# The projection of the second attention branch, rebuilt around single-operand work on VectorE

## The chip, the cores and the metric

The kernel runs on one core of a Trainium2 chip. The engines that matter are TensorE (PE, the matmuls; PEld is its weight load), VectorE (DVE), ScalarE (ACT), GpSimd (POOL) and SyncE (SP), which here issues most of the DMAs; ACT issues the rest from its own instruction stream. SBUF is the on-chip memory that all engines read and write; PSUM is the memory, in eight banks, into which TensorE accumulates. The metric is the device time of one execution in microseconds.

## The reference

One layer of a streaming encoder: 1024 prompt frames and 64 sample frames (1088 columns in all, written T below) of 1024 channels.

```python
h = rms_norm(x, norm_w) @ w_in          # 6144 columns: q, k, v, z of two branches, then g_sb, g_cb
b_sb = (o_sb * silu(z_sb)) @ w_proj_sb  # o_sb: stick-breaking attention, 8 heads x 64
b_cb = (o_cb * silu(z_cb)) @ w_proj_cb  # o_cb: chunk-band attention, 8 heads x 64
y = x + (sigmoid(g_sb) * b_sb + sigmoid(g_cb) * b_cb) @ w_out
```

The first branch is called sb, the second cb. Each projection has 512 input channels and 1024 output channels. All values are float32.

## The kernel before

**Arithmetic.** TensorE multiplies a rounded 32-bit type (fp32r). Each float32 operand x is therefore split into a high part xh (x rounded, written by ACT as a copy) and a low part xl = x - xh (a subtraction on DVE or POOL), and each product is three matmuls: whi by xh, whi by xl, wlo by xh. The parts of a weight block are made by `W.split`: high by ACT (L107), low by POOL (L114).

**Stages.** The input projection comes first (matmuls at L453, and L622 in products of half-size blocks). Then attention: for every stick-breaking or chunk-band tile TensorE makes scores (L994, L995), transposes weights (L1046) and multiplies values (L1085), while ACT takes exponentials (L1004) and DVE normalises (L1018) and copies transposes out of PSUM (L1057). TensorE would idle between these, so a generator hands it "fill" matmuls in between: first the last units of the input projection (L758, with their gate columns g_sb and g_cb passing through ACT, L733, and to DRAM, L675), and then the sb projection (L883), whose results DVE multiplies by the gate (L888). The order within each engine is the order in which the code is written; a tile framework adds the waits. `fill(n)` hands out n further matmuls, or all that are left.

**The two projections.** One generator, `proj_units`, does both. It walks 24 steps: output unit pair i (0 to 3), column chunk ci (`CH`: 384, 384 and 320 of the T columns) and unit uu (0, 1). A unit is 128 output channels. Each step is 12 matmuls into one PSUM tile. For sb the pair is (2i, 2i+1), for cb it is (i, i+4). The gates come back from DRAM in tiles of one unit, 128x384, issued from ACT's stream (L842), three or seven steps ahead; the sb gates are already sigmoids, those of cb get their sigmoid on ACT (L847). For sb the product goes from PSUM into `tbt`, the sum of both branches (1024 channels by T). For cb DVE multiplies PSUM by the gate into SBUF (L891), POOL adds that onto `tbt` (L892), and then the parts for the output projection are made: `keep_h` makes high (ACT, L911) and low (DVE, L913) of the finished columns, three steps behind.

**Sums.** The output projection (matmuls L1337) multiplies by `w_out` in two column halves i, each as seven block products and one b step instead of eight, in the order `OP_`. It needs differences of quarters of `tbt`. `sums_h(k)` makes four of them for the channel pair k: differences into an SBUF tile d (DVE, L923), high part (ACT, L924), low part (DVE, L928). k = 0, 1 run during cb; k = 2, 3 after it. The block weights are made by `prep_o` (ACT L1236, low part on POOL or DVE L1237, sums of weight blocks L1220, L1228). The 64 sample columns take their own matmuls (L1372) from `hs` (L1264, L1265). Results leave by L1360 and L1294.

**Memory.** `x` and its parts live in four tiles of 128x4xT; when x is dead, `tbt` and the parts of the merged value take their places. The cb input (attention output times gate, parts `og`) is made from `ot` tiles loaded by SP (L813) with ACT L817 and DVE or POOL L822. In PSUM the cb units use two banks of `acc` and four of `b`.

Of the kernel before, what the change touches and what calls it, by code (L numbers as in the profile page):

```python
# [17 lines left out]
KT = 8  # L18
# [14 lines left out]
def hybrid_step_kernel(ctx: ExitStack, tc: tile.TileContext, x_prompt, x_sample, c_sbk, c_sbv, c_cbk, c_cbv,  # L33
# [94 lines left out]
    xhl = [[xpool.tile([128, 4, T], F32R, name=f"x{s}{h}") for h in range(2)] for s in "hl"]  # L128
# [622 lines left out]
    def run_fill():  # L751
        for j, (kind, c, args) in enumerate(units):
            wh, wl = W.sp.pop(("u", j))
            for ci, (a, b) in enumerate(CH):
                ps = psF.tile([128, 512], F32, name="acc")
                for k in range(KT):
                    for n, (w, x) in enumerate(((wh, 0), (wh, 1), (wl, 0))):
                        TE.matmul(ps[:, :b - a], w[:, k], xk(x, k)[:, a:b], start=k == 0 and n == 0,  # L758
                                  stop=k == KT - 1 and n == 2)
                        if ci == k == n == 0 and j + 1 == len(units):  # L760
                            load_og("sb", 0, late["y"])
                        if ci == 1 and k == 0 and n == 0:
# [13 lines left out]
        late["tbt"] = [xpool.tile([128, 4, T], F32, name=f"x{s}1") for s in "hl"]  # L776
        late["tbx"] = ExitStack()
        late["tbp"] = late["tbx"].enter_context(tc.tile_pool(name="tbp", bufs=1, side="right"))
        g = proj_units("sb", late["tbp"], 4)
        next(g)  # L780
        next(g)
        for i, v in enumerate(g):
            yield v
            og_step(i % 3 == 2)
# [3 lines left out]
    def og(b, s, p):  # L788
        return xk(s, p) if b == "sb" else late["og"][s][:, p]

    def tb(u):
        return late["tbt"][u // 4][:, u % 4]
# [16 lines left out]
    def load_og(b, ci, stage, ps=range(NPAIR)):  # L809
        a, e = CH[ci]  # L810
        for p in ps:
            ots[ci, p] = stage.tile([128, 384], F32, name="ot", bufs=4)
# [17 lines left out]
    def proj_units(b, pool, ng):  # L830
        gts = {}
        pair = [(2 * i, 2 * i + 1) if b == "sb" else (i, i + 4) for i in range(KT // 2)]
        order = [(i, uu, ci) for i in range(KT // 2) for ci in range(3) for uu in range(2)]

        def load_g(x):
            if x < len(order):
                i, uu, ci = order[x]
                u = pair[i][uu]
                a, e = CH[ci]
                gts[x] = (late["y"].tile([128, 384], F32, name="ot", bufs=4) if b == "cb" and x & 4  # L840
                          else pool.tile([128, 384], F32, name="gt", bufs=4))
                A.dma_start(gts[x][:, :e - a], d_g[b][u][:, a:e])  # L842

        def sig(x):
            if b == "cb" and x < len(order):
                a, e = CH[order[x][2]]
                A.activation(gts[x][:, :e - a], gts[x][:, :e - a], AF.Sigmoid)  # L847

        nxt = [0]

        def load_to(n):
            while nxt[0] < n:
                load_g(nxt[0])
                nxt[0] += 1

        load_to(min(ng - 1, 4))
        yield 0
        if b == "cb":
            W.split(("p", 5))
        sig(0)  # L860
        yield 0
        for x, (i, uu, ci) in enumerate(order):
            u = pair[i][uu]
            i += 0 if b == "sb" else 4
            wh, wl = W.sp["p", i]
            a, e = CH[ci]
            n = e - a
            cw = slice(uu * 128, uu * 128 + 128)
            if x % 6 == 0:
                load_proj(i + 2)  # L870
            if x % 6 == 0 and i != 4:
                if i + 1 < 8:
                    W.split(("p", i + 1))
                else:
                    late["o"](0)
            sig(x + 1)
            gt = gts.pop(x)
            nm = [None, None, "b20", "b21", "b30", "b31"][x % 6] if b == "cb" else None
            ps = late["psB"].tile([128, 512], F32, name=nm) if nm else psF.tile([128, 512], F32, name="acc")
            for p in range(NPAIR):  # L880
                gh, gl = og(b, 0, p), og(b, 1, p)
                for m, (w, g) in enumerate(((wh, gh), (wh, gl), (wl, gh))):
                    TE.matmul(ps[:, :n], w[:, p, cw], g[:, a:e], start=p == 0 and m == 0,  # L883
                              stop=p == NPAIR - 1 and m == 2)
                    if p < NPAIR - 1 or m < 2:
                        yield 1
            if b == "sb":
                V.tensor_tensor(out=tb(u)[:, a:e], in0=ps[:, :n], in1=gt[:, :n], op=OP.mult)  # L888
            else:
                h = tb(u)  # L890
                V.tensor_tensor(out=gt[:, :n], in0=ps[:, :n], in1=gt[:, :n], op=OP.mult)  # L891
                G.tensor_tensor(out=h[:, a:e], in0=gt[:, :n], in1=h[:, a:e], op=OP.add)  # L892
                keep.append((u, a, e))
                if len(keep) > 3:
                    keep_h(1, *keep.pop(0))
                if len(keep) > 1:
                    keep_h(0, *keep[-2])
                if x > 7:
                    next(late["t"][(x - 2) // 6 - 1], None)
            load_to(x + ng)  # L900
            yield 1

    keep = []

    def keep_h(s, u, a, e):

        hh, hlo = late["h"][u // 4]
        f = tb(u)
        z = min(e, NP if u >= 4 else 512)
        if a < z and s == 0:  # L910
            A.activation(hh[:, u % 4, a:z], f[:, a:z], AF.Copy)  # L911
# [510 lines left out]
```

## Time and profile before

| What | Value |
|---|---|
| three timed runs, median (lowest to highest) | 1038.21 us (1035.22 to 1039.8) |
| the profiled execution | 1038.12 us, its span 1036.3 us |
| busy TensorE | 996.2 us, 96% of the span |
| busy VectorE | 672.3 us, 65% |
| busy ScalarE / GpSimd | 475.6 us, 46% / 330.1 us, 32% |
| granted TensorE clock, mean | 0.988 |
| DMA | 164.20 MB, mean 158 GB/s |

The span is what the profiler saw of the engines; 1.8 us of the execution lie around it. Times within the profile count from the span's start. In rows of the trace a name such as `gt` is a tile, `d_gsb` a buffer in DRAM; "out<-in" names what an instruction writes and reads. After a row, "[1.9 <-ACT wT L1055]" is the idle time ahead of it on its engine and the instruction that ended it.

### The profile page before, as it was taken

To read this page: it belongs to the slowest core of one execution; us is meant where nothing else is said; L and a number is where in the kernel's file an instruction comes from. 1 tells how busy PE (TensorE), PEld (TensorE's weight loads), DVE (VectorE), ACT (ScalarE), POOL (GpSimd) and SP (SyncE) were. 2 spreads that over 40 slices of the span, in tenths; PEclk is the share of its full clock that TensorE was granted. 3 is DMA by queue.
4 is the path that set the end of the run, shared out by engine and by line. 5 is a ranking of instruction groups with operands and counts; after the bars stand their busy time and mean duration, and the time that the engine had idled before them with its cause. 6 is when DMAs were issued, how large, how long until landed. Compare 5 with 4: busy or idle time off the path is not lost.

```text
span 1036.3 us, 20146 instructions
## 1 busy us (share of the span) xinstructions
PE 996.2 (96%) x7512; PEld 947.9 (91%) x7512; DVE 672.3 (65%) x1246; ACT 475.6 (46%) x1088; POOL 330.1 (32%) x342
## 2 busy tenths in 40 slices
PE   5999999999999999999999999999999999976998
PEld 5999999998999999988989798998988898976998
DVE  5466663885345554198989787566667773799644
ACT  5544432443343333376767575444445433644220
POOL 3376662114354442211111111101004002765632
PEclk9999999999999999999999999999999999998999
DMA  7636468335555332885665474565757635530632
GB/s 239 205 128 207 160 230 285 118 93 163 160 162 177 95 96 85 214 206 156 164 156 159 130 191 135 172 173 166 196 138 226 175 98 175 163 111 29 196 124 80
DMA packets 176114, 164.20 MB, mean 158 GB/s; under 512 B 34512, under 2 KB 162384, under 8 KB 175888
## 3 DMA queue, kind: packets, MB, share of 16 engines
q1 hardware_dynamic: 160384, 145.67, 47.3%
q10 hardware_dynamic: 15632, 17.24, 5.4%
q8 instruction: 59, 0.97, 0.4%
q14 instruction: 39, 0.32, 0.1%
HBM read 104.14 MB, written 58.72 MB: 157 GB/s over the span
## 4 chain that ended last, share of the span: by engine, by line
PE 87%; DVE 6%; DMA 3%; issue 1%; ACT 1%; POOL 1%; SPq 0%; ACTq 0%; DVEq 0%; POOLq 0%
PE acc L453 18%; PE acc L758 17%; PE b L622 15%; PE o L1085 7%; PE b L1337 7%; PE pt L1046 6%; PE acc L883 6%; PE z L995 3%; PE z L994 3%; PE b L883 2%; DVE kp L1014 1%; DMA out_dram<-kos 1%; DMA wrawx<-in_w_in_dram 1%; DVE be L1015 1%; PE pk L338 1%
## 5 line engine op out<-in xcount | busy, mean ns | idle before, releaser
L114 POOL TENSOR_TENSOR wlo<-wraw,whi 128x1024 fp32r<-128x1024 f32 x31 | 75.9, 2449 | 257.0 <-ACT whi L107 220.8
L758 PE MATMUL acc<-xh,wlo 128*128 128x384 f32 (+1 forms) x384 | 130.9, 341 | 0.0
L758 PE MATMUL acc<-xh,whi 128*128 128x384 f32 (+1 forms) x384 | 130.4, 340 | 0.0
L758 PE MATMUL acc<-xl,whi 128*128 128x384 f32 (+1 forms) x384 | 128.6, 335 | 0.0
L1014 DVE TENSOR_TENSOR_SCAN kp<-kp,imp 64x576 f32<-64x576 f32 (+8 forms) x72 | 102.7, 1427 | 21.7 <-ACT kp L997 21.5
L1004 ACT ACTIVATE be<-be,sm 128x640 f32<-128x640 f32 (+5 forms) x72 | 50.7, 705 | 99.9 <-DVE sm L1000 99.9
L1046 PE MATMUL pt<-ident,be 128*128 128x128 f32 (+2 forms) x608 | 90.6, 273 | 6.2 <-DVE wT L1057 3.3
L1055 ACT ACTIVATE wT<-pt 128x512 f32<-128x512 f32 (+3 forms) x130 | 63.5, 502 | 53.8 <-PE pt L1046 53.7
L1046 PEld LDWEIGHTS pt<-ident,be 128*128 128x128 f32 (+2 forms) x608 | 68.8, 140 | 18.2 <-issue 6.4
L453 PE MATMUL acc<-whi,xh 128*128 128x256 f32 x256 | 74.7, 294 | 0.0
L758 PEld LDWEIGHTS acc<-xh,whi 128*128 128x128 f32 x384 | 72.9, 190 | 1.6
L758 PEld LDWEIGHTS acc<-xh,wlo 128*128 128x128 f32 x384 | 72.7, 189 | 1.1
L758 PEld LDWEIGHTS acc<-xl,whi 128*128 128x128 f32 x384 | 72.3, 188 | 0.9
L453 PE MATMUL acc<-wlo,xh 128*128 128x256 f32 x256 | 71.2, 280 | 0.0
L453 PE MATMUL acc<-wlox,xh 128*128 128x256 f32 x256 | 71.2, 280 | 0.0
L453 PE MATMUL acc<-whi,xl 128*128 128x256 f32 x256 | 71.2, 280 | 0.0
L453 PE MATMUL acc<-whix,xh 128*128 128x256 f32 x256 | 71.2, 280 | 0.0
L453 PE MATMUL acc<-whix,xl 128*128 128x256 f32 x256 | 71.1, 280 | 0.0
L1015 DVE TENSOR_TENSOR be<-be,kp 64x576 f32<-64x576 f32 (+8 forms) x72 | 60.3, 837 | 9.6
L997 ACT ACTIVATE kp<-z 128x384 f32<-128x384 f32 (+6 forms) x112 | 54.3, 484 | 24.7 <-PE z L995 23.2
L1085 PE MATMUL o<-wT,vp 128*64 128x256 f32 (+1 forms) x608 | 65.5, 356 | 0.0
L1085 PEld LDWEIGHTS o<-wT,vp 128*64 128x64 f32 x608 | 42.1, 136 | 22.9 <-issue 7.0
(327 smaller groups left out, 3011.8 us busy)
## 6 DMA issues: line engine op xcount, KB each, us to landing
wraw<-in_w_in_dram SPq DMA_DIRECT2D x35, 512.0 KB, 4.4
wrawx<-in_w_in_dram SPq DMA_DIRECT2D x13, 512.0 KB, 4.5
sq<-d_qsbT SPq DMA_DIRECT2D x32, 192.0 KB, 4.2
sq<-d_qcbT SPq DMA_DIRECT2D x32, 192.0 KB, 4.0
xt<-in_x_prompt_dram SPq DMA_DIRECT2D x8, 512.0 KB, 5.4
d_kcbT<-hl SPq DMA_DIRECT2D x8, 512.0 KB, 4.4
d_qcbT<-hl SPq DMA_DIRECT2D x8, 512.0 KB, 5.5
d_ksbT<-hl SPq DMA_DIRECT2D x16, 256.0 KB, 2.6
```

The lines of the kernel that those rows point to most:

```text
L114: (eng or G).tensor_tensor(out=l, in0=raw, in1=h[:].bitcast(F32), op=OP.subtract)
L453: TE.matmul(ps, x, w, start=m == 0, stop=m == len(steps) - 1)
L622: TE.matmul(ps[:, :m], w[:, hl_, k], right[s](x)[:, k, a:b], start=s < 3 and k == 0 and e == 0, stop=k == 3 and e == 2, skip_group_check=s ...
L758: TE.matmul(ps[:, :b - a], w[:, k], xk(x, k)[:, a:b], start=k == 0 and n == 0, stop=k == KT - 1 and n == 2)
L883: TE.matmul(ps[:, :n], w[:, p, cw], g[:, a:e], start=p == 0 and m == 0, stop=p == NPAIR - 1 and m == 2)
L997: A.activation(kp[:r, x:y], z[:r, :m], AF.Sigmoid, scale=-0.125)
L1014: V.tensor_tensor_scan(kp[:r, n - 1::-1], kp[:r, n - 1::-1], im[:, ::-1], 0.0, op0=OP.mult, op1=OP.add)
L1015: V.tensor_tensor(out=be[:r, :n], in0=be[:r, :n], in1=kp[:r, 1:n + 1], op=OP.mult)
L1046: TE.transpose(pt[:kr, x, :r], be[:r, kb * 128:kb * 128 + kr], ident[:r, :r])
L1055: A.activation(w[:, sl:sl + m, q0:q0 + r], pt[:, :m, :r], AF.Copy)
L1085: TE.matmul(o[hd * 64:hd * 64 + 64, c0:c1], vv[:kr, kb, hd * 64:hd * 64 + 64], wT[b, p, j, hd, s // 4][:kr, s % 4, c0:c1], start=si == 0, ...
L1337: TE.matmul(ps[:, t], left[s](xs_)[:, k, ts_], wt_[:, k], start=s < 3 and t == k == e == 0, stop=k == 3 and e == 2, skip_group_check=s > 2 ...
```

## The change

What it does, part by part:

1. **Layout.** The middle two of the four x tiles become one (`xm`), so `tbt` is one tile of 8 units and one operation can cover the units i and i+4. The sb input's parts move to the outer two tiles.
2. **sb.** `proj_sb` walks 12 chunks j = (i, ci) of two units each. The gates come as one tile [128, 2, 384], two buffers, issued by SP (L841) and not by ACT. `load(j + 1)` stands twice in a chunk, at its start and after its first unit; both copies go into one buffer, so the second waits for the first. The weights of the next pair are split in the chunk ci = 1, and not in ci = 0.
3. **cb.** `proj_cb(j)` does a chunk of two units. For ci = 1 and 2 both units lie in one PSUM tile of two banks. DVE multiplies by the gate in place, in PSUM (L910), and then adds `tbt` itself (L911, one operand from PSUM); for ci = 1, 2 each covers two units (128x2x384, 128x2x320). POOL's addition is gone. Gates: two units a tile, four chunks ahead, issued by SP; the sigmoid covers two units.
4. **Low parts.** `keep_lo` (L933) is on POOL, one chunk behind.
5. **Sums.** `sums_h` writes its differences into PSUM. The first two (L950) have both operands in SBUF, the other two (L954, L955) and the four low parts (L947) have one operand in PSUM. k = 0 to 2 run from chunk 3 to 11, k = 3 in `last_sums`, behind the first block product of the output projection.
6. **Weights.** The low part of the second cb weight block goes to DVE. The block sums of the first half of `w_out` are made by POOL (L1284, L1286) in chunks 1 and 2. `OP_` swaps its third and fourth entry; `hs` is one operation of ACT and one of POOL.

The matmuls of TensorE are the same in number. The diff, cut to its core:

```diff
+        load_gate(late["tbp"], "gt", 0, d_g["sb"][0:2], 0)
-        g = proj_units("sb", late["tbp"], 4)
+        late["tbt"] = xpool.tile([128, KT, T], F32, name="xm")
+        for i, v in enumerate(proj_sb(late["tbp"])):
...
+    def load_gate(pool, name, key, us, ci):
+        a, e = CH[ci]
+        gts[key] = pool.tile([128, 2, 384], F32, name=name, bufs=2)
+        for w, d in enumerate(us):
+            SP.dma_start(gts[key][:, w, :e - a], d[:, a:e])
+
+    def proj_sb(pool):
+        load = lambda j: j < 12 and load_gate(pool, "gt", j, d_g["sb"][2 * (j // 3):2 * (j // 3) + 2], j % 3)
+        for j in range(12):
...
+            load(j + 1)
+            if ci == 0:
+                load_proj(i + 2)
+            if ci == 1:
+                W.split(("p", i + 1))
...
+                V.tensor_tensor(out=tb(2 * i + uu)[:, a:e], in0=ps[:, :e - a], in1=gt[:, uu, :e - a], op=OP.mult)
+                if uu == 0:
+                    load(j + 1)
...
+        if ci:
+            ps = late["psB"].tile([128, 2, 512], F32, name=f"b{ci + 1}")
...
+        h = late["tbt"][:, i:i + 5:4, a:e]
+        for x, y, o in (((ps[:, :, :n], gt[:, :, :n], h),) if ci else
+                        [(pp[uu][:, :n], gt[:, uu, :n], h[:, uu]) for uu in range(2)]):
+            V.tensor_tensor(out=x, in0=x, in1=y, op=OP.mult)
+            V.tensor_tensor(out=o, in0=x, in1=o, op=OP.add)
+        load_gcb(j + 4)
-                V.tensor_tensor(out=gt[:, :n], in0=ps[:, :n], in1=gt[:, :n], op=OP.mult)
-                G.tensor_tensor(out=h[:, a:e], in0=gt[:, :n], in1=h[:, a:e], op=OP.add)
...
+                G.tensor_tensor(out=hl, in0=f, in1=hh.bitcast(F32), op=OP.subtract)
-            V.tensor_tensor(out=hlo[:, u % 4, a:z], in0=f[:, a:z], in1=hh[:, u % 4, a:z].bitcast(F32),
-                            op=OP.subtract)
...
     def sums_h(k):
+        d = [psF.tile([128, 512], F32, name="acc")[:] for _ in range(2)]
-            d[n] = late["hp"].tile([128, 512], F32, name="d", bufs=2)
...
+        for j in range(2):
+            V.tensor_tensor(out=d[j], in0=x(j, 1), in1=x(0, j), op=OP.subtract)
+        high(0)
+        yield
+        low(0)
+        V.tensor_tensor(out=d[1], in0=x(1, 1), in1=d[0], op=OP.subtract)
+        V.tensor_tensor(out=d[0], in0=x(1, 0), in1=d[1], op=OP.subtract)
+        yield
+        high(2)
+        yield
+        low(2)
...
-    OP_ = [0, 3, 1, 2, 4, "b", 5, 6]
+    OP_ = [0, 3, 2, 1, 4, "b", 5, 6]
...
+    for j in range(12):
+        proj_cb(j)
+        if j == 0:
+            W.split(("p", 5), V)
+        if j == 1:
+            G.tensor_tensor(out=wsum[3], in0=wsum[0], in1=wsum[1], op=OP.add)
+        if j == 2:
+            G.tensor_tensor(out=wsum[2], in0=wsum[3], in1=wsum[2], op=OP.subtract)
+        if j:
+            keep_lo(j - 1)
+        if j == 11:
+            prep_o(1)
+        else:
+            keep_hi(j)
+        if j > 2:
+            if j % 3 == 0:
+                tjobs = sums_h(j // 3 - 1)
+            if j < 11:
+                next(tjobs, None)
+            if j in (4, 7):
+                next(tjobs)
...
+    def last_sums():
...
+        t3 = sums_h(3)
+        for _ in range(3):
+            next(t3)
+        prep_o(3)
+        keep_hi(11)
+        keep_lo(11)
```

The order of DVE in the middle of the cb projection, before, from the first gate product of a chunk on. `gt` is a gate tile, `b` a PSUM tile with a unit's matmuls, `xl` and `xh` with a number are halves of `tbt` or parts, `h0l` a low part, `d` a difference and th0 to th3 the parts of the differences.

```order
L891 TENSOR_TENSOR gt<-b_11582,gt 128x384
L913 TENSOR_TENSOR h0l<-xh_10320,h0h 128x384
L928 TENSOR_TENSOR th0l<-d,th0h 128x512
L923 TENSOR_TENSOR d<-xl_10321,d 128x512
L891 TENSOR_TENSOR gt<-b_11606,gt 128x320
L913 TENSOR_TENSOR xl_11376<-xl_10321,xh_11375 128x384
L928 TENSOR_TENSOR th1l<-d,th1h 128x512
L923 TENSOR_TENSOR d<-xl_10321,xh_10320 128x512
L891 TENSOR_TENSOR gt<-b_11630,gt 128x320
L913 TENSOR_TENSOR h0l<-xh_10320,h0h 128x128
L928 TENSOR_TENSOR th3l<-d,th3h 128x512
L891 TENSOR_TENSOR ot<-acc,ot 128x384
```

The same place in the change; here `xm` is `tbt`, and `acc` is a PSUM tile with a difference. Two units share an operation, the low parts of the finished columns are gone from DVE, and the additions onto `tbt` and the subtractions with PSUM are there:

```order
L910 TENSOR_TENSOR b_11526<-b_11526,ot 128x384
L911 TENSOR_TENSOR xm<-b_11526,xm 128x384
L910 TENSOR_TENSOR b_11527<-b_11527,ot 128x384
L911 TENSOR_TENSOR xm<-b_11527,xm 128x384
L950 TENSOR_TENSOR acc<-xm 128x512 x2
L910 TENSOR_TENSOR b_11569<-b_11569,gt 128x2x384
L911 TENSOR_TENSOR xm<-b_11569,xm 128x2x384
L947 TENSOR_TENSOR tk_11203<-acc,tk_11203 128x512 x2
L954 TENSOR_TENSOR acc<-xm,acc 128x512
L955 TENSOR_TENSOR acc<-xm,acc 128x512
L910 TENSOR_TENSOR b_11610<-b_11610,gt 128x2x320
L911 TENSOR_TENSOR xm<-b_11610,xm 128x2x320
```

Before, a gate product and low parts alternate, and all but the products have both operands in SBUF; now only the two L950 have.

The gate loads of the sb projection stood in ACT's order before, between the work of attention (L817 copies of the attention output, L1055 copies of transposes, L1004 exponentials) and the weight split (L107):

```order
L842 DMA gt<-d_gsb_93 128x384
L842 DMA gt<-d_gsb_94 128x384
L842 DMA gt<-d_gsb_93 128x384
L107 ACTIVATE whi<-wraw 128x1024
L1055 ACTIVATE wT<-pt 128x3x128
L817 ACTIVATE xh_139<-ot 128x320
L1004 ACTIVATE be,sm<-be,sm 128x640
L817 ACTIVATE xh_139<-ot 128x320
L842 DMA gt<-d_gsb_94 128x384
L1055 ACTIVATE wT<-pt 128x3x128
L817 ACTIVATE xh_139<-ot 128x320
L1004 ACTIVATE be,sm<-be,sm 128x640
```

In the change they stand in SP's order, among the loads of weights (L805) and of the attention's gate `zt` (L1081) and the store of its result (L678). In brackets are the semaphores that an instruction waits for (DMAHW: an earlier transfer has landed; DVE: VectorE has come so far):

```order
L841 DMA gt_10838<-d_gsb4_97 128x384 [waits DMAHW3_49,DMAHW2_49,DVE_49]
L841 DMA gt_10838<-d_gsb5_98 128x384
L841 DMA gt_10874<-d_gsb4_97 128x384 [waits DMAHW4_49,DMAHW3_49,DMAHW2_49]
L841 DMA gt_10874<-d_gsb5_98 128x384
L1081 DMA zt_10890<-d_zcb3_92 128x256
L841 DMA gt_10912<-d_gsb4_97 128x384 [waits DMAHW7_49,DMAHW0_49,DVE_49]
L841 DMA gt_10912<-d_gsb5_98 128x384
L805 DMA wraw_10915<-in_w_proj_cb_dram 128x4x128 [waits DMAHW1_49,Pool_49]
L805 DMA wraw_10915<-in_w_proj_cb_dram 128x4x128
L841 DMA gt_10966<-d_gsb4_97 128x384 [waits DMAHW7_49,DMAHW0_49]
L841 DMA gt_10966<-d_gsb5_98 128x384 [waits DMAHW4_49]
L678 DMA d_ocb3_116<-zt_10744 128x256 [waits DMAHW5_49,DVE_49]
```

Every gate tile is named twice, once for each of the two `load` calls; the second pair waits for the transfers of the first, and what stands behind it on SP waits too.

More of the change, by code (lines that the diff above doesn't have):

```diff
@@ L828, in make_og @@
             og_lo(b, ci, p)
[L830 to L864, printed above, removed]
@@ L880, in proj_units @@
             for p in range(NPAIR):
-                gh, gl = og(b, 0, p), og(b, 1, p)
+                gh, gl = og("cb", 0, p), og("cb", 1, p)
                 for m, (w, g) in enumerate(((wh, gh), (wh, gl), (wl, gh))):
[L883 to L899, printed above, removed]
```

249 lines of the change are left out of this document (144 added, 105 removed).

## The prediction

> **What bounds the kernel now.** I read the table of windows first, by rounds of the cb projection, then TensorE's waits and the chain of waits behind it, then VectorE's groups there. A row of windows gives start:end, length, busy time (and instructions) of PE, PEld, DVE, ACT, POOL, then granted clock, DMA share and GB/s.
>
> ```profile
> 877.70:889.60 11.90, 11.89 (x72) 11.90 (x73) 4.21 (x7) 6.49 (x12) 6.62 (x6) 1.00 0.77 235
> 889.60:901.50 11.90, 11.90 (x74) 11.90 (x73) 10.27 (x16) 7.38 (x17) 10.91 (x9) 1.00 0.55 164
> 901.50:913.50 12.00, 12.00 (x75) 12.00 (x74) 11.93 (x14) 5.73 (x13) 6.58 (x6) 1.00 0.34 104
> 913.50:925.20 11.70, 11.70 (x73) 11.70 (x72) 11.60 (x17) 6.12 (x13) 5.57 (x6) 1.00 0.25 75
> 925.20:956.60 31.40, 17.82 (x117) 16.21 (x115) 30.84 (x33) 13.33 (x26) 16.61 (x11) 0.83 0.16 53
> 956.60:1032.40 75.80, 75.78 (x622) 75.57 (x622) 41.30 (x49) 15.11 (x18) 33.26 (x13) 0.98 0.42 135
> ```
>
> Four rounds of cb keep TensorE full. But from the third on VectorE is full too, and when the rounds end at 925.2 it is still busy to 956.6, while TensorE works 17.82 of 31.40 us at a clock of 0.83. TensorE's waits after 870 us (total, times, longest) say for what:
>
> ```profile
> PE b L1337 <- ACT whio L1236: 4.4, 1, 4.4
> PE b L1337 <- DVE h0l L913: 4.3, 1, 4.3
> PE b L1337 <- POOL wlo L1237: 2.4, 2, 1.8
> ```
>
> ACT had been free before whio; the chain (start, length, what) shows VectorE ahead of it:
>
> ```profile
> 940.98 5.17 DVE xl L913 x2
> 946.15 2.87 DVE hs L1265 x2
> 953.72 0.51 issue
> 954.23 1.05 ACT whio L1236
> 955.31 1.24 DVE wloo L1237
> 956.59 18.58 PE b L1337 x142
> 975.17 0.96 PE acc L1372 x8
> 982.85 11.39 PE b L1337 x96
> 1032.41 0.69 DVE xl L1360
> ```
>
> So the stretch is set by VectorE's backlog. **Its worth:** at full clock a block matmul takes 11.39/96 = 0.1187 us, so 117 of them are 13.9 of the 31.4 us: 17.5 lost. The next 142 took 18.58 where 16.9 would do: 1.7 more. Ceiling 19.2 us. Before 925.2 and behind it TensorE is full, so there is nothing else there.
>
> How the backlog grows is seen from two windows of VectorE, each one round long by its rows:
>
> ```profile
> 901.30:917.70 16.40, 16.30 (x21) 1.00 0.33 100
> 917.70:934.00 16.30, 16.20 (x21) 0.84 0.31 98
> ```
>
> A round costs VectorE 16.3 us and TensorE 11.85 (47.5/4): 4.45 us behind per round. Why so dear is in its groups (busy, mean ns):
>
> ```profile
> L913 DVE TENSOR_TENSOR xl<-xl,xh 128x384 fp32r<-128x384 f32 x8 | 11.4, 1425 | 0.0
> L923 DVE TENSOR_TENSOR d<-xh 128x512 f32<-128x512 f32 x4 | 5.2, 1290 | 0.0
> L928 DVE TENSOR_TENSOR th0l<-d,th0h 128x512 fp32r<-128x512 f32 x4 | 5.2, 1300 | 0.0
> L923 DVE TENSOR_TENSOR d<-xl,xh 128x512 f32<-128x512 f32 x4 | 2.8, 693 | 0.1
> L891 DVE TENSOR_TENSOR gt<-acc,gt 128x384 f32<-128x384 f32 x4 | 2.1, 545 | 0.0
> L891 DVE TENSOR_TENSOR gt<-b,gt 128x320 f32<-128x320 f32 x4 | 1.9, 483 | 0.0
> 917.23 0.55 DVE L913 TENSOR_TENSOR h0l<-xh,h0h 128x384 fp32r<-128x384 f32 x1
> L892 POOL TENSOR_TENSOR xl<-ot,xl 128x384 f32<-128x384 f32 x4 | 5.0, 1246 | 4.7 <-DVE ot L891 4.7
> L114 POOL TENSOR_TENSOR wlo<-wraw,whi 128x1024 fp32r<-128x1024 f32 x3 | 7.2, 2399 | 7.1 <-ACT whi L107 5.3 <-POOL xl L892 1.0 <-DMA gt<-d_gcb 0.8
> ```
>
> The same 384-wide subtraction takes 0.55 us (917.23) or a mean of 1.43; the 512-wide ones 0.69 or 1.3; at 940.98 two L913 took 5.17, about when POOL made weight parts. Those that stretch have two operands in SBUF. The gate products L891, one operand in PSUM, stay at 0.48 to 0.55 in every group.
>
> **A second loss** lies in attention, at 793 us. The windows, then what ACT and TensorE did:
>
> ```profile
> 793.00:796.00 3.00, 1.09 (x8) 0.85 (x7) 0.56 (x2) 2.21 (x4) 1.08 (x1) 0.95 1.09 226
> 796.00:799.00 3.00, 3.00 (x11) 3.00 (x11) 0.56 (x1) 0.47 (x3) 2.12 (x2) 0.50 0.89 272
> 793.41 0.33 ACTq L842 DMA_DIRECT2D gt<-d_gsb  x1
> 793.79 1.06 ACT L107 ACTIVATE whi<-wraw 128x1024 fp32r<-128x1024 f32 x1 [1.66 <-DMA sq<-d_qcbT]
> 795.27 0.44 PE L1046 MATMUL pt<-ident,be 128*128 128x128 f32 x2 [1.91 <-ACT wT L1055]
> 796.19 0.56 DVE L888 TENSOR_TENSOR xh<-acc,gt 128x384 f32<-128x384 f32 x1 [2.49 <-DMA gt<-d_gsb]
> ```
>
> A gate load in ACT's stream waited for a transfer, behind it the weight split and the copy wT, and TensorE for that: 1.9 us idle, then 3.0 us at half clock (1.5 lost): 3.4 us.
>
> **The change part by part.** *VectorE's round of cb.* Removed: five L913 and the eight L923 and L928 in SBUF. New, from chunk 3 on: four 384-wide operations with PSUM (two products, two additions) at 0.545, as L891; two of 768 and two of 640 elements; six 512-wide with one PSUM operand; two L950 with both in SBUF. From L891 at 320 (0.483) to 512 at 0.69 the slope is about 1.09 ns an element, so 768 take 0.97 and 640 take 0.83. Sum 4 x 0.545 + 2 x 0.97 + 2 x 0.83 + 8 x 0.69 = 11.3 us if nothing stretches; with the L950 at L923's 1.29 it is 12.5. No row shows an operation whose result goes to PSUM; nothing excludes that it is as quick as one to SBUF (11.3), and were each of the 14 with PSUM some 0.3 us dearer the round would be 16.3 again. I take 11.9, near the lower end since the nearest rows, L891, never stretched. That equals TensorE's 11.85, so the backlog no longer grows, and the 19.2 us go. The first round, without sums, is 5.8 us: a reserve.
>
> [...]
>
> *POOL* loses its six L892 a round and gets the low parts: three of 384 columns, one of 256 and one of 128, some 5 us by L892's rate (1.25 for 384), and a weight part of 2.4: 7.5 of 11.85, so the cover is ample. It also makes two block sums of some 2.5 us in the first round; both hide there.
>
> *Weight part on DVE in the first round*, 1.23 us as L1237 or 2.5 beside POOL. It stands behind chunk 0 and is wanted at the second round, 12 us on: cost 0 to 2.5, taken 0.5.
>
> *The end of cb.* The last sums (k = 3), the last low parts and the weight part 3 are made behind the last cb matmul. A block takes 48 matmuls, 5.7 us; by `OP_` the fourth, s = 1, is the first to need them all, three blocks and the samples (1.9, twice the 0.96 of the chain) later: 19.0 us. The chain to it: VectorE's tail of the last chunk, ACT's copy of the first block at 5.7, then highs and lows in turn (0.69 each at least on VectorE, two by two, with ACT between), the weight's high 1.05 and its low 2.4 on POOL: by these rows 17 to 20. Cost 0 to 3, taken 0.5.
>
> *The gates of sb on SP.* The 3.4 us at 793 go, as ACT no longer holds a gate load and the first gate is loaded in the last input unit. But each later chunk is loaded twice, and the second copy waits on SP for the first. What is queued behind it are the attention's own loads, and VectorE waits at L865 for both copies. Rows that price it:
>
> ```profile
> 800.23 2.19 SPq L713 DMA_DIRECT2D vs<-d_cbv  x1
> 806.65 0.54 DVE L888 TENSOR_TENSOR xh<-acc,gt 128x384 f32<-128x384 f32 x1
> 857.88 0.49 DVE L888 TENSOR_TENSOR xl<-acc,gt 128x320 f32<-128x320 f32 x1
> gt<-d_gsb ACTq DMA_DIRECT2D x13, 192.0 KB, 2.5
> vs<-in_cache_cb_v_dram SPq DMA_DIRECT2D x1, 256.0 KB, 7.0
> ```
>
> A gate lands 2.5 us after issue. SP is fullest at 797 to 810 (a single issue held it 2.19). Two copies, one behind the other, and four issues (0.33 at 793.41) there put the gates of chunks 1 and 2 at about 805 to 808, while their products were due at 803 to 807; VectorE would be held some 2.6 us twice, with attention's copies behind it, of which TensorE loses 0 to 5. I take 3, nearer the stall at 793, where a hold of ACT of 1.66 cost 3.4. Later a chunk lasts TensorE (857.88 - 796.19)/8 = 7.7 us: enough for two copies.
>
> *Moved at no cost:* the split to ci = 1, hidden by a chunk of 7.7 us (else 2.4 for the part); `OP_`, the single `hs` operation and the merged sigmoid, hidden by ACT at 6 of 12 us a round.
>
> **Sum**, against the profiled execution of 1038.1 us, 0.1 under the median, its span and 1.8 around it: 1038.1 - 19.2 - 3.4 + 0.5 + 0.5 + 3 = **1019.5 us**. By the bounds: all costs nothing 1015.5; all at their upper ends (2.5 + 3 + 5) 1026, and with a round of 12.5, three times 0.65 late, 1028.
>
> **The rivals.** *VectorE still sets the rounds.* If L950 and others stretch to make a round 13.5 to 14.5 us, three rounds leave 5 to 8 us of backlog, and TensorE's clock drops again: 1024.5 to 1029, with the taken costs near their ends 1031. For it: 11.9 has no slack, POOL now makes low parts in the same time. Against: only two of 16 operations can stretch by the rows.
>
> *The second gate copy becomes the bound: slower.* A chunk of sb cannot be shorter than two landings, one behind the other, for there are two buffers: with issue about 1.1 us plus the landing L of the second from when the first is down. At 2.5 that is 3.6 us if the first was issued early, below 7.7 and below the 3.95 of the last four chunks, which TensorE runs alone. But attention's own loads took up to 7.0 us to land in this stretch. At L = 7 eight chunks cost max(0, 8.1 - 7.7) and four 8.1 - 3.95 each: 3 + 17 = 20, all of the gain; that is the point from which it decides. At 8 it is 11 + 21 = 32, and 1052. Against: the 13 gate loads here had a median of 2.5.
>
> *The change doesn't do what it says.* Operations with PSUM stretch too when TensorE is writing other banks or when their result goes there, and a round stays at 16.3: 13.4 of backlog come back, and 1.7 of slow clock: 1034 to 1036.
>
> **How the numbers follow.** Forecast with its costs (1015 to 1024): 0.60. Below 1015, more gone than I saw: 0.09. VectorE still the bound (1024 to 1032): 0.18. No effect: 0.06. Slower by gates: 0.07. What a measurement can tell from no change is 0.5%, 5.2 us: faster below 1033.0, 0.87; within 0.06; slower above 1043.4, 0.07. The range of 1014 to 1031 leaves out no effect and the slower case (0.13) and a little at either end, some 0.05.
>
> **What would show it.** Right: TensorE full from the first cb matmul to the end, no L1337 wait above 2 us, clock 1.00; L910 and L911 at 0.55, 0.83 and 0.97 without spread; a VectorE round of 11.3 to 12.5. The step on the weight part is wrong if TensorE waits for it at the second round, the one on the end of cb if it waits there for a sum or a weight part. The gate step shows in VectorE's L865 waiting for `gt`: twice at about 804 and 808 by my sum, in every chunk by the slower rival. What would make it wrong: a price for PSUM results, which no row shows, and landings under SP's new load.

## The result

| | before | the change |
|---|---|---|
| median (lowest to highest) | 1036.72 us (1034.26 to 1039.8, 4 runs) | 1023.06 us (1021.39 to 1026.16, 4 runs) |
| profiled execution, span | 1038.12 us, 1036.3 us | 1022.21 us, 1020.3 us |
| granted clock, mean | 0.988 | 0.997 |
| busy VectorE / GpSimd | 672.3 / 330.1 us | 654.5 / 322.3 us |

The ratio is 0.987 (95% interval 0.9831 to 0.9909): faster by 13.7 us. The forecast was 1019.5, with a range of 1014 to 1031.

The span falls into pieces at three first matmuls of TensorE: of the sb projection, of cb, and of the output projection. These four numbers are read from the first starts of those lines in each trace, and are used for every run below.

| stretch, us | before | the change | difference |
|---|---|---|---|
| start to first sb matmul | 788.9 | 788.3 | -0.6 |
| sb and the end of attention | 88.8 | 88.4 | -0.4 |
| cb projection | 47.5 | 50.0 | +2.5 |
| output projection to the end | 111.1 | 93.6 | -17.5 |

The first row is not touched by the change; over all runs here it lies between 785.1 and 789.5, so the span of a single profile says little below some 4 us, and the stretches are compared one by one.

The windows of the change, from the first cb matmul on, answer to the first table of the prediction (start:end, length, busy time and instructions of PE, PEld, DVE, ACT, POOL, clock, DMA share, GB/s):

```profile
876.70:890.85 14.15, 12.66 (x76) 12.09 (x74) 7.07 (x11) 7.33 (x12) 4.04 (x5) 1.00 0.86 273
890.85:902.72 11.87, 11.30 (x69) 11.31 (x69) 11.10 (x15) 7.57 (x14) 11.87 (x8) 1.00 0.81 248
902.72:914.58 11.86, 11.86 (x75) 11.86 (x73) 11.65 (x17) 7.41 (x13) 10.47 (x11) 1.00 0.45 140
914.58:926.70 12.12, 12.12 (x76) 12.12 (x75) 11.88 (x18) 7.40 (x13) 7.66 (x7) 1.00 0.18 52
926.70:947.36 20.66, 19.25 (x162) 19.05 (x160) 14.31 (x18) 8.49 (x14) 10.21 (x6) 1.00 0.29 96
947.36:1016.40 69.04, 69.04 (x576) 68.83 (x576) 37.65 (x47) 14.72 (x17) 28.24 (x11) 1.00 0.45 144
```

TensorE no longer falls behind VectorE: the stretch after cb, which took 31.4 us at a clock of 0.83, is gone. VectorE is still full in the rounds (11.65 of 11.86), but it ends them together with TensorE. What TensorE still waits for after 870 us, in all:

```profile
PE b L1394 <- DVE fl L1436: 1.4, 1, 1.4
PE b L905 <- DVE wlo L114: 1.1, 1, 1.1
PE b L905 <- ACT whi L107: 1.0, 1, 1.0
PE acc L861 <- DVE xm L865: 0.5, 1, 0.5
```

VectorE's groups in cb (885 to 930 us; busy, mean ns of one) are the ones that the prediction priced:

```profile
L950 DVE TENSOR_TENSOR acc<-xm 128x512 f32<-128x512 f32 x6 | 7.1, 1226 | 0.0
L947 DVE TENSOR_TENSOR tk<-acc,tk 128x512 fp32r<-128x512 f32 x10 | 6.4, 680 | 0.0
L911 DVE TENSOR_TENSOR xm<-b,xm 128x384 f32<-128x384 f32 x8 | 4.5, 557 | 0.3
L911 DVE TENSOR_TENSOR xm<-b,xm 128x768 f32<-128x768 f32 x4 | 3.8, 957 | 0.1
L911 DVE TENSOR_TENSOR xm<-b,xm 128x640 f32<-128x640 f32 x4 | 3.3, 825 | 0.1
L910 DVE TENSOR_TENSOR b<-b,ot 128x384 f32<-128x384 f32 x4 | 2.2, 556 | 0.0
```

Whatever has an operand in PSUM takes 0.56, 0.68, 0.83 and 0.96 us for 384, 512, 640 and 768 elements. Only L950, with both operands in SBUF, is stretched, to a mean of 1.23; in low_on_dve below, with POOL nearly empty, it is 0.69. In the change's trace TensorE's matmuls write only PSUM tiles, and no row of POOL names a PSUM tile.

### The profile page after: what moved, and what is told of

Same layout as the page of the kernel before. It is cut to its first block, busy times and chain, and to the rows that moved or that the text cites. A ratio compares the mean times of both kernels' runs of the same rounds, so it can differ in the third digit from the quotient of the medians.

```text
span 1020.3 us, 20165 instructions
## 1 busy us (share of the span) xinstructions
PE 990.5 (97%) x7512; PEld 942.2 (92%) x7512; DVE 654.5 (64%) x1233; ACT 473.7 (46%) x1075; POOL 322.3 (32%) x338
## 5 line engine op out<-in xcount | busy, mean ns | idle before, releaser
L114 POOL TENSOR_TENSOR wlo<-wraw,whi 128x1024 fp32r<-128x1024 f32 x30 | 73.9, 2465 | 246.4 <-ACT whi L107 211.3
L761 PE MATMUL acc<-xm,whi 128*128 128x384 f32 (+1 forms) x384 | 129.1, 337 | 0.0
L456 PE MATMUL acc<-whi,xa 128*128 128x256 f32 x256 | 74.7, 294 | 0.0
L761 PEld LDWEIGHTS acc<-xm,whi 128*128 128x128 f32 x384 | 72.5, 189 | 1.0
L456 PE MATMUL acc<-wlo,xa 128*128 128x256 f32 x256 | 71.2, 280 | 0.0
L456 PE MATMUL acc<-wlox,xm 128*128 128x256 f32 x256 | 71.2, 280 | 0.0
L456 PE MATMUL acc<-whi,xm 128*128 128x256 f32 x256 | 71.2, 280 | 0.0
L456 PE MATMUL acc<-whix,xm 128*128 128x256 f32 x256 | 71.2, 280 | 0.0
L456 PE MATMUL acc<-whix,xb 128*128 128x256 f32 x256 | 71.1, 280 | 0.0
L761 PE MATMUL acc<-xa,wlo 128*128 128x384 f32 (+1 forms) x192 | 65.6, 342 | 0.0
L761 PE MATMUL acc<-xa,whi 128*128 128x384 f32 (+1 forms) x192 | 65.6, 342 | 0.0
```

The source lines that it names most:

```text
L114: (eng or G).tensor_tensor(out=l, in0=raw, in1=h[:].bitcast(F32), op=OP.subtract)
L456: TE.matmul(ps, x, w, start=m == 0, stop=m == len(steps) - 1)
```

## The experiments

Two things were to be told apart. Where the gain comes from: my theory is that VectorE's operations with one operand in PSUM are not held up by POOL's work; the rivals are that there are fewer and wider operations, or that POOL simply took work off a full VectorE. And where the three losses come from (2.5 us in cb, the wait for `fl`, and the 3.4 us near 793 that were to go): the second copies of the gates, or something else. All runs below, with the stretches of their profiled execution:

| run | median, us | ratio to before, 95% | sb | cb | output |
|---|---|---|---|---|---|
| the change | 1023.06 | 0.987 (0.9831 to 0.9909) | 88.4 | 50.0 | 93.6 |
| sbuf_product | 1030.8 | 0.9941 (0.9922 to 0.996) | 88.7 | 53.6 | 101.6 |
| sbuf_pool_idle | 1025.48, one run | | 88.8 | 53.7 | 92.0 |
| low_on_dve | 1027.04 | 0.9915 (0.9892 to 0.9937) | 88.2 | 49.1 | 100.0 |
| one_unit | 1023.99 | 0.9871 (0.9849 to 0.9893) | 88.1 | 48.4 | 98.3 |
| one_copy | 1018.57 | 0.9816 (0.9799 to 0.9832) | 88.4 | 47.4 | 93.5 |
| early_split | 1019.01 | 0.9822 (0.9808 to 0.9837) | 88.8 | 49.1 | 93.6 |
| end_swap | 1019.6 | 0.9826 (0.9799 to 0.9853) | 88.0 | 49.5 | 91.8 |
| before_sp (before, one edit) | 1038.6 | 1.0019 (1.0003 to 1.0035) | 89.1 | 47.6 | 110.9 |
| swap_and_one_copy | 1015.9 | 0.9803 (0.9782 to 0.9825) | 87.0 | 47.4 | 91.7 |
| split_on_dve | 1019.42 | 0.9822 (0.98 to 0.9845) | 90.1 | 48.0 | 91.7 |

The change was not timed again beside its variants. The medians of one_copy, early_split, end_swap and swap_and_one_copy lie 1 to 3 us further below it than their cb and output stretches account for, so a difference of medians from the change is read here no finer than some 3 us, and the stretches carry the argument.

### The product in SBUF

```diff
-            V.tensor_tensor(out=x, in0=x, in1=y, op=OP.mult)
-            V.tensor_tensor(out=o, in0=x, in1=o, op=OP.add)
+            V.tensor_tensor(out=y, in0=x, in1=y, op=OP.mult)
+            V.tensor_tensor(out=o, in0=y, in1=o, op=OP.add)
```

> The gate product of cb goes into the gate tile in SBUF, so the addition behind it has two SBUF operands; number and width of the operations are as in the change. If what keeps VectorE quick is the one operand in PSUM, the additions stretch (mean of 384, 768, 640 columns above 0.7, 1.3 and 1.1 us instead of 0.56, 0.97, 0.83), a round of cb takes VectorE 13 to 15 us instead of 11.86, and three rounds late cost 3 to 9 us: 1026 to 1032. If it is that there are fewer and wider operations, the durations stay and the time is 1023 within 1.5.

Measured: 1030.8 us, 7.7 above the change (the profiled execution was the slowest of the four, 1034.54, so its stretches add up to more). The output stretch takes 101.6 instead of 93.6, since VectorE comes out of cb with a backlog again: its round takes 14.44 us (the products at 913.99 and 928.43) instead of 11.86, within the 13 to 15 expected. Its groups (888 to 930 us):

```profile
L911 DVE TENSOR_TENSOR xm<-ot,xm 128x384 f32<-128x384 f32 x4 | 6.7, 1666 | 0.1
L911 DVE TENSOR_TENSOR xm<-gt,xm 128x384 f32<-128x384 f32 x3 | 3.8, 1280 | 0.1
L910 DVE TENSOR_TENSOR ot<-b,ot 128x384 f32<-128x384 f32 x4 | 2.2, 546 | 0.0
L114 DVE TENSOR_TENSOR wlo<-wraw,whi 128x1024 fp32r<-128x1024 f32 x1 | 3.4, 3364 | 0.0
```

The product, still read from PSUM, stays at 0.55; the addition behind it, same width and same number, goes from 0.56 to 1.3 and 1.7. So width and number, which are the same here, are not what keeps the addition short. (The weight part L114 also went from 1.2 to 3.4 us and held TensorE 3.2 us, 2.1 more than in the change. That is 2.1 of the 3.6 us by which cb is longer; single matmuls of cb also take up to 0.52 us, 0.44 in the change, and the mean granted clock of the execution is 0.991 instead of 0.997.)

### The same, with POOL nearly idle

```diff
             V.tensor_tensor(out=y, in0=x, in1=y, op=OP.mult)
             V.tensor_tensor(out=o, in0=y, in1=o, op=OP.add)
...
-                G.tensor_tensor(out=hl, in0=f, in1=hh.bitcast(F32), op=OP.subtract)
+                A.activation(hl, f, AF.Copy)
```

> As the run with the gate product in SBUF, but POOL's low parts are left out of cb: ACT writes a copy in their place (the low parts are wrong by it; all else is computed). POOL is then left with a weight part of 2.4 us a round. If it is POOL's work that stretches operations with two SBUF operands, the additions fall back to 0.6 to 0.8, 1.0 and 0.9 us on the mean for 384, 768 and 640 columns. If SBUF operands are slow by themselves, they stay at 1.3 to 1.7 for 384.

The mean for 384 fell to 0.99 only, between the two theories' numbers, but single rows decide it (start, length, engine and line; first VectorE, then POOL's only operation there):

```profile
912.74 0.56 DVE L911 TENSOR_TENSOR xm<-ot,xm 128x384 f32<-128x384 f32 x1
913.81 2.27 DVE L911 TENSOR_TENSOR xm<-ot,xm 128x384 f32<-128x384 f32 x1
925.09 0.56 DVE L911 TENSOR_TENSOR xm<-gt,xm 128x384 f32<-128x384 f32 x1
926.15 2.26 DVE L911 TENSOR_TENSOR xm<-gt,xm 128x384 f32<-128x384 f32 x1
```

```profile
913.26 2.40 POOL L114 TENSOR_TENSOR wlo<-wraw,whi 128x1024 fp32r<-128x1024 f32 x1 [9.47 <-ACT whi L107]
925.60 2.40 POOL L1259 TENSOR_TENSOR wlo<-wraw,whi 128x1024 fp32r<-128x1024 f32 x1 [9.94 <-ACT whi L1258]
```

Without POOL the two-operand addition takes 0.56, as long as one with PSUM. If it starts while POOL runs, it ends 0.4 us after POOL does (916.08 behind 915.66, 928.41 behind 928.00): it is not slowed, it is held until POOL's operation is over. The products and additions of the change, with an operand in PSUM, are not held: the 32 in cb (L910, L911) lie between 0.555 and 0.967 us, each at the length of its width. Two rows of the change show a product that starts and ends inside the same kind of weight part on POOL:

```profile
919.41 2.41 POOL L1259 TENSOR_TENSOR wlo<-wraw,whi 128x1024 fp32r<-128x1024 f32 x1 [3.97 <-ACT whi L1258]
920.00 0.56 DVE L910 TENSOR_TENSOR b<-b,gt 128x384 f32<-128x384 f32 x1
```

So it is POOL's work, 2.27 us beside it against 0.56 without, and for these operations only where both operands are in SBUF; in the output stretch, 92.0, TensorE no longer waits for VectorE.

### Low parts on VectorE

```diff
-                G.tensor_tensor(out=hl, in0=f, in1=hh.bitcast(F32), op=OP.subtract)
+                V.tensor_tensor(out=hl, in0=f, in1=hh.bitcast(F32), op=OP.subtract)
```

> The change with the low parts of the finished columns on VectorE again, in place of POOL. VectorE had no idle time in rounds 2 to 4 of cb (11.86 us each); five operations with two SBUF operands add 2.5 us a round if they don't stretch (POOL then has only the weight parts) and 5 if they stretch: 3 rounds, 7 to 15 us of backlog, and TensorE waits for it in the output projection: 1030 to 1038. If VectorE was not the bound, as it is 64% busy, the time stays at 1023 within 1.5.

VectorE's groups, 888 to 930 us, and TensorE's waits:

```profile
L933 DVE TENSOR_TENSOR xb<-xm,xa 128x384 fp32r<-128x384 f32 x7 | 6.1, 866 | 0.0
L950 DVE TENSOR_TENSOR acc<-xm 128x512 f32<-128x512 f32 x6 | 3.9, 690 | 0.0
```

```profile
PE b L1394 <- DVE h0l L933: 3.0, 2, 2.6
PE b L1394 <- DVE fl L1436: 2.7, 1, 2.7
```

1027.04, 4.0 above the change and under the range of 1030 to 1038; the output stretch grows by 6.4 us. A settled round of VectorE takes 12.59 us (the products at 909.89 and 922.48) instead of 11.86. The five low parts of that round take 2.35 us, as expected, but with POOL nearly empty the pair of L950 falls from 2.46 to 1.29, which gives 1.2 us a round back; that was left out of the expectation. More of the delay comes from two low parts that POOL's block sum and weight part held in the first rounds: 2.75 us (at 891.32) instead of 0.55, and 1.46 (at 898.39) instead of 0.42. The mean granted clock of the execution is 0.996, against 0.997. So VectorE is the bound of these rounds and has no slack, as its 64% over the whole span would not tell.

### One unit per operation

```diff
-        for x, y, o in (((ps[:, :, :n], gt[:, :, :n], h),) if ci else
-                        [(pp[uu][:, :n], gt[:, uu, :n], h[:, uu]) for uu in range(2)]):
+        for x, y, o in [(pp[uu][:, :n], gt[:, uu, :n], h[:, uu]) for uu in range(2)]:
```

> The change with one unit per operation for all chunks (four more products and four more additions a round, each half as wide). By the trace two of 384 take 1.12 (start to start 1.06) for one of 768 at 0.97 (0.93), two of 320 some 0.96 for one of 640 at 0.83: a round is 0.4 to 0.6 us longer for VectorE, which has no idle time in rounds 2 to 4, so 1.2 to 1.8 us come late and 0 to 2 us are lost: 1023 to 1025. If the width was the main gain, and not the PSUM operand, it is 5 us or more.

The median is 0.9 above the change, with intervals that cover each other. The stretches say more: output 98.3 instead of 93.6 (TensorE's wait for `fl` is 3.2 instead of 1.4), cb 48.4 instead of 50.0. The durations are as expected: a settled round of VectorE takes 12.49 us (the products at 905.55 and 918.04) instead of 11.86. But the first pair of differences with two SBUF operands (L950, here L949) was held by POOL for longer, 4.35 us instead of 2.19; the later pairs take no more than in the change (2.35 against 2.46). The first two pairs, and TensorE's wait:

```profile
893.20 4.35 DVE L949 TENSOR_TENSOR acc<-xm 128x512 f32<-128x512 f32 x2
907.68 2.35 DVE L949 TENSOR_TENSOR acc<-xm 128x512 f32<-128x512 f32 x2
```

```profile
PE b L1393 <- DVE fl L1435: 3.2, 1, 3.2
```

Two units an operation is worth some 3 us in these two stretches together, and 2.2 us of VectorE's lateness is that one pair; the medians bound it between about nothing and 3. It is not the main gain.

### One copy of each gate

```diff
                 V.tensor_tensor(out=tb(2 * i + uu)[:, a:e], in0=ps[:, :e - a], in1=gt[:, uu, :e - a], op=OP.mult)
-                if uu == 0:
-                    load(j + 1)
```

> Each sb gate chunk is loaded once (the second load call is gone), all else as in the change. If the double copies cause what the mixed stage lost again between 796 and 811 us (2.75 us), that comes back, VectorE's 2.0 us wait for a gate near 872 goes, and the time falls by 3 to 5 us against the change (1018 to 1020). If the loss at 804 to 807 is instead a normalisation that ran beside the weight split, TensorE's waits of 0.96 and 0.69 stay where they are, only the hold near 872 goes (TensorE 0.45), and the loads for cb come earlier: 0.5 to 2.9 us.

1018.57, 4.5 below the change: the number of the first theory, but by luck, for what happens is what the second one says. The normalisation still takes 2.62 us (at 801.40), TensorE's hold of 0.45 us at 873 goes, and the loads for cb come earlier. The sb stretch is 88.4 in both. That does not show that the second copies cost nothing there, since this profile has a wait of 1.87 us near 790 that the change's lacks, and behind it, from 792.33 to 794.25, matmuls of 384 columns that start 0.32 us apart instead of 0.18 (more on that wait below). What falls is cb, by 2.6 us, to the 47.4 of before. The two rows of ACT that tell why, of the change and then of this run:

```profile
885.84 1.28 ACT L880 ACT_TABLE_LOAD   x1 [3.32 <-DMA gt<-d_gcb]
888.62 1.04 ACT L107 ACTIVATE whi<-wraw 128x1024 fp32r<-128x1024 f32 x1
```

```profile
881.20 1.28 ACT L878 ACT_TABLE_LOAD   x1 [1.59 <-DMA gt<-d_gcb]
883.98 1.04 ACT L107 ACTIVATE whi<-wraw 128x1024 fp32r<-128x1024 f32 x1
```

The cb gates stand on SP behind the last copies of sb's and behind the loads of the cb input; ACT takes the first sigmoid before the split of the next weights, and VectorE the low part behind chunk 0. In the change the whole chain runs 4.6 us later (3.4 if counted from the first cb matmul): the first cb gates are issued 2.5 us later on SP (879.79 against 877.27), and they also take longer to land (6.0 us from that issue to ACT's start, against 3.9), which no run here explains. So TensorE stands at the second round for the high part (0.95 us) and the low part (1.10).

### The split ahead of the first sigmoid

```diff
+    W.split(("p", 5), V)
     sig(0)
...
-        if j == 0:
-            W.split(("p", 5), V)
```

> The split of the second cb weight block stands ahead of the first sigmoid and not behind chunk 0. If it was late only because ACT took the sigmoid of a late gate first, TensorE's waits of 0.95 (high part) and 1.10 (low part) at the second round go: 2.0 to 2.4 us faster than the change. If the late gate itself sets the round, TensorE waits a little later for a PSUM bank of chunk 0 or 1, and 0 to 1 us is gained.

Both waits go, but another takes part of their place, one round on (TensorE's row, and POOL's that stands behind it):

```profile
902.07 0.45 PE L905 MATMUL b<-og,wlo 128*128 128x384 f32 x1 [1.43 <-POOL wlo L114]
```

```profile
890.67 2.39 POOL L1283 TENSOR_TENSOR wo<-wo,wo 128x1024 f32<-128x1024 f32 x1 [7.87 <-DMA wo<-in_w_out_dram]
```

POOL's first block sum waits for a load that stands still further back on SP, and the next weight part waits for POOL. cb takes 49.1: 0.9 gained, not 2.0 to 2.4. The lateness is that of SP's queue, and moving one customer of it ahead only shows the next one. (The median, 1019.01, is 4 us below the change, outside both expectations; the stretches do not show where the rest comes from.)

### The last parts ahead of the weight

```diff
-        prep_o(3)
         keep_hi(11)
         keep_lo(11)
+        prep_o(3)
```

> In the last sums the parts of chunk 11 are made ahead of weight part 3. If the chain behind TensorE's wait is low part of chunk 11, then output addition, sample addition, bank, then the wait of 1.41 goes and the slow block behind it (0.46): 1.9 us faster. If the weight part comes too late by it, TensorE waits for that instead, 0 to 2 us: no gain.

The rows of the change that stand behind its wait, in order of time:

```profile
941.60 2.41 POOL L1259 TENSOR_TENSOR wo<-wo,wo 128x1024 fp32r<-128x1024 f32 x1 [5.51 <-ACT wo L1258]
943.96 0.74 POOL L933 TENSOR_TENSOR xb<-xm,xa 128x256 fp32r<-128x256 f32 x1
944.73 1.29 DVE L1419 TENSOR_TENSOR xm<-b,xr 128x512 f32<-128x512 f32 x2 [3.33 <-POOL xb L933]
946.89 0.42 DVE L1436 TENSOR_TENSOR fl<-b,fl 64x256 f32<-64x256 f32 x1 [0.87 <-ACT fl L1435]
```

VectorE's output addition L1419 writes where `tbt` was, so it waits for the last reader of `tbt`, the low part of chunk 11 on POOL, which stood behind the weight part. With the two exchanged the wait is gone and the output stretch is 91.8: 1.8 us, as expected (1.9). (The median is 3.5 below the change, more than that.)

### Before, with the sb gates on SP

```diff
-                A.dma_start(gts[x][:, :e - a], d_g[b][u][:, a:e])
+                (SP if b == "sb" else A).dma_start(gts[x][:, :e - a], d_g[b][u][:, a:e])
```

> The kernel before, with one edit: the sb gate loads are issued by SP and not from ACT's stream. By the prediction's step (a gate load in ACT's stream was what held TensorE near 793) the stall of 3.4 us goes and sb plus attention, from the first sb matmul to the first of cb, takes 85.4 instead of 88.8 us: 1034.5. By what the four runs so far show (88.0 to 88.8 with the gates on SP, and TensorE waiting near 790 behind ACT's copy of a late attention output) the stretch stays at 88 to 89 and the time is that of before within 1.5.

1038.6 us, ratio 1.0019: no gain. TensorE's 1.9 us behind ACT go, and 3.0 behind VectorE come, three microseconds on. The granted clock behind the wait is 0.51 from 799 to 802, as it was 0.50 from 796 to 799 in the kernel before:

```profile
798.03 0.56 DVE L888 TENSOR_TENSOR xh<-acc,gt 128x384 f32<-128x384 f32 x1 [4.84 <-DMA gt<-d_gsb]
798.65 0.44 PE L883 MATMUL acc<-xh,whi 128*128 128x384 f32 x1 [3.02 <-DVE xh L888]
```

The gates, now behind SP's other loads, are late for VectorE. In the change they are not, since the first one is loaded in the last input unit; yet its sb stretch is as long. Two other delays are there. In seven of the ten profiles of the change and its variants (not in the change itself, one_unit and swap_and_one_copy) TensorE waits 1.06 to 1.87 us between 788 and 793, behind ACT, which waits for a load of the attention output; ACT's row and TensorE's in the run with one copy:

```profile
788.95 0.52 ACT L822 ACTIVATE xa<-ot 128x384 fp32r<-128x384 f32 x1 [2.46 <-DMA ot<-d_osb]
790.01 0.44 PE L1062 MATMUL pt<-ident,be 128*128 128x128 f32 x2 [1.87 <-ACT wT L1071]
```

And in the change, at 802, a normalisation of attention meets POOL's weight part, which the change has moved there, and TensorE waits for what VectorE does behind it (in seven of the nine variants too, 0.47 to 0.97 us):

```profile
801.81 2.38 POOL L114 TENSOR_TENSOR wlo<-wraw,whi 128x1024 fp32r<-128x1024 f32 x1 [3.81 <-ACT whi L107]
801.95 2.59 DVE L1036 TENSOR_SCALAR be<-be,sm 128x640 f32<-128x640 f32 x1
804.97 0.34 PE L1012 MATMUL z<-kss,sqs 128*64 128x288 f32 x1 [0.96 <-DVE sm L1018]
```

### Both repairs, and a third that failed

swap_and_one_copy joins the edits of one_copy and end_swap.

> The change with each gate loaded once and with the parts of chunk 11 ahead of weight part 3. If the two losses are separate (2.4 us at the second round of cb, 1.75 at the end), they add: cb in 47.5 and the output projection in 88.0 us, together 4.2 us faster than the change, 1017 to 1018. If the one hides the other, the time is that of one alone, 1018.5 to 1019.5.

1015.9 us, 7 below the change and 1 below the range expected, ratio 0.9803 to before. cb 47.4 and output 91.7: both repairs are there in full (the 88.0 expected for the output is a slip: 93.6 less 1.75 is 91.9). TensorE has no wait above 1 us left from 785 us on:

```profile
PE z L1010 <- DVE sm L1016: 1.0, 1, 1.0
PE pt L1062 <- DVE wT L1073: 0.6, 2, 0.4
PE pt L1062 <- ACT wT L1071: 0.5, 2, 0.4
```

The sb stretch, 87.0, is the shortest of all runs. The single copy accounts for the 0.45 us at 873. The run with one copy alone had 88.4 with a wait of 1.87 near 790 that this profile lacks, so I take the rest for the spread of that stretch and not for a gain, which is argued and not shown. split_on_dve adds to it:

```diff
-                W.split(("p", i + 1))
+                W.split(("p", i + 1), V)
```

> One copy, the swap at the end, and the low weight parts of sb on VectorE and not on POOL. If the normalisation that took 2.59 us at 802 was held by POOL's weight part (801.81 to 804.19), it takes 0.55 again and TensorE's wait of 1.0 us behind it goes; VectorE pays 1.1 us three times in a stage where it is 69% busy. Between 0.5 and 1.5 us faster than the run with one copy and the swap, if VectorE's 1.1 us lie beside fill; else 0 to 1 slower. The normalisation's longest duration tells the mechanism whatever the time does.

A miss: 1019.42. The normalisation falls from 2.59 to 0.55 and its wait goes, as the mechanism has it, but VectorE's copies of transposes stand behind the 1.2 us of the weight part, and the wait near 790 is there again:

```profile
805.95 0.55 DVE L1034 TENSOR_SCALAR be<-be,sm 128x640 f32<-128x640 f32 x1
```

```profile
PE pt L1062 <- ACT wT L1071: 2.1, 2, 1.7
PE pt L1062 <- DVE wT L1073: 2.0, 4, 0.7
```

The sb stretch is 90.1, 3.1 above the run without it. 1.7 of that is the wait near 790, which comes and goes; VectorE's copies of transposes hold TensorE 1.4 us more, against 1.0 saved; the remaining 1 us is not placed. So the step gains nothing, and whether it loses lies within the two intervals (0.9782 to 0.9825 against 0.98 to 0.9845).

## Why the prediction was right, and where it was not

The forecast was 1019.5. The profiled execution came out at 1022.2, 2.7 above it, and the median at 1023.06. Term by term:

- **VectorE's backlog, -19.2: right, in mechanism and size.** The round was priced at 11.3 to 12.5 and taken as 11.9; it starts every 11.86 us (the products at 907.07 and 918.93) and holds 11.65 us of work. The three widths were given as 0.545, 0.97 and 0.83 and came out at 0.56, 0.96 and 0.83; L950 was bounded by 1.29 and came out at 1.23. The unknown price, that of a result in PSUM, is nothing that a row shows: 0.56 for 384 (L910), against 0.55 with the result in SBUF (L891 before). The output stretch fell by 17.5; with the 1.8 that the end of cb cost, below, that is 19.3. sbuf_product and sbuf_pool_idle show the cause as predicted: operations stretch that have two operands in SBUF beside POOL (2.27 instead of 0.56). low_on_dve shows that moving the low parts to POOL is part of the gain.
- **Weight part of the first round, +0.5: mis-sized, and for another reason.** Measured +2.5. I let it stand between 0 and 2.5 for VectorE's own duration beside POOL; that was 1.22, as cheap as hoped, but by luck: it started at 890.14, 0.17 us ahead of POOL's block sum (890.31). In sbuf_product it started at 890.87, behind POOL's 890.60, and took 3.36. What I didn't follow was its way to VectorE: ACT's first sigmoid ahead of it, the cb gate ahead of that, and SP's queue ahead of the gate. one_copy shows it.
- **End of cb, +0.5: mis-sized.** Measured 1.8 (93.6 against 91.8 with the swap), inside the 0 to 3 given. The chain was named up to the weight part and the low part; its last link, the output addition that waits for `tbt`'s last reader and the sample addition that holds a PSUM bank, was not.
- **The stall at 793, -3.4, and late gates, +3: right in sum by luck, wrong in how the terms come about.** Together they were -0.4 and the stretch shows -0.4. The stall is gone in the change, but before_sp shows that the loads' place in ACT's stream was not a cause that could be taken away by itself: there the stall moved to VectorE. The 3 us did not come back through late gates at 804 and 808, where VectorE waits for none; the only such hold of TensorE is the 0.45 us at 873. In the change's profile 1.65 us came back as a normalisation held by POOL (TensorE's 0.96 at 804.97, and 0.69 behind it), which the weight split had brought there; I had put that move down as free. In most of the other profiles the wait near 790 comes on top. The rest is not placed.

Of the rivals, "VectorE still sets the rounds" was the near one: it has no slack, and one_unit shows what half a microsecond more a round does. "No effect" is refuted by the L910 and L911 rows. The slower side, gates that can't land twice within a chunk, didn't come: 192 KB landed in a median of 2.7 us over the whole trace, and one such wait is there (0.5 us of TensorE near 873), in the stretch that TensorE runs alone, where that rival's margin was smallest.

## What to carry to other kernels

Where VectorE and POOL work side by side, count VectorE's operations with two SBUF operands, and give them one operand in PSUM before making them fewer: here 384 elements beside POOL's weight part took 2.27 us with both operands in SBUF (sbuf_pool_idle), and 0.56 with one in PSUM (the change). A result in PSUM costs VectorE no more time here (0.56 against 0.55). Of a term that is "hidden", follow the chain that leads to it through every queue (here SP, then ACT, then VectorE), since the engine that does the work was not what was late. And a step moved onto an idle engine can hold the busy one, as the weight part on POOL did the normalisation (2.59 us instead of 0.55): ask what runs beside it at the new place.

## What was not expected

- A held VectorE operation is not stretched in proportion. Its end lies behind that of POOL's operation by nearly its own length: 0.42 us for 384 elements (0.56 alone), 0.82 for 768 (0.96 alone), 1.09 for 1024 (1.22 alone). The hold also goes the other way: POOL's block sum below, 2.4 us when nothing is in its way, started while VectorE's weight part ran (to 894.61) and took 3.24. Both rows are of sbuf_pool_idle; VectorE's ends at 897.66, 0.82 us behind POOL's 896.84:

```profile
893.60 3.24 POOL L1286 TENSOR_TENSOR wo<-wo,wo 128x1024 f32<-128x1024 f32 x1
895.51 2.15 DVE L911 TENSOR_TENSOR xm<-gt,xm 128x768 f32<-128x768 f32 x1
```

  So by these rows what a hold costs is about what is left of the other engine's operation. Whether several short operations of POOL do less harm than one long one of the same sum was not tried.
- The normalisation L1036 reads one tensor from SBUF and beside it only one value a partition, and it is held too, 2.59 instead of 0.55. One operand in SBUF is not by itself safe; here it was so for operations whose other operand is in PSUM (0.56 for 384 elements).
- SP's queue order reached TensorE four hops away: the last second copy was issued at 875, and TensorE stood until 889.7.

What stays open: the wait near 790, which is there in seven profiles and not in three, behind loads of the attention output; what makes these late was not tried. What the second copies cost sb beyond 0.45 us, since that wait hides it. And how much of the gain is that of the sums in PSUM alone: a run with their differences in SBUF, for which I saw no room left there, was not made.
